# A two-layer decoder trunk on one core: another order of the opening, and other places for the modulation tiles

## The chip, the cores and the metric

One core of one Trainium2 chip runs the whole kernel. The metric is the device time of one execution in microseconds. Before the change the median of 3 runs was 2732.73 us (2731.3 to 2734.19).

## What is computed

1024 tokens of width 1024 pass two layers and a final RMSNorm; everything is float32. Cut to what matters here:

```python
c_act = silu(c)                                   # one vector of 1024
for l in range(2):
    mod = c_act @ w_ada[l] + b_ada[l]             # 6144 values per layer
    sh1, sc1, g1, sh2, sc2, g2 = split(mod, 6)
    h = rms_norm(x, ln1_g[l]) * (1 + sc1) + sh1
    z = h @ w_in[l]                               # pool input, q and kv latents, rope key, two gates
    y_a = pool_mixer(...) @ p_pool[l]
    y_b = mla(..., cos, sin) @ p_attn[l]          # 8 heads, causal
    x = x + g1 * ((sigmoid(gz_a) * y_a + sigmoid(gz_b) * y_b) @ w_out[l])
    h2 = rms_norm(x, ln2_g[l]) * (1 + sc2) + sh2
    x = x + g2 * (relu(h2 @ w_ff1[l])**2 @ w_ff2[l])
return rms_norm(x, final_g)
```

## The kernel before

Activations lie with the features on the 128 partitions: `x` is 8 tiles (k) of 128 x 1024, each in two halves c of 512 tokens. Every dense product is made of three TensorE (PE) matmuls per 128x128x512 block, since each operand is split into a high part (ScalarE cast, ACT) and a low part (a subtraction, mostly on VectorE, DVE): `split` (L305, L306) for activations, `w_split` (L254, L256) for weights. PE matmuls are recorded at L292, those of the second feed-forward product at L1235.

**Modulation tiles.** The 2 x 48 column groups of `w_ada` are tiles of 128x1024 (512 KB). `ada_tile` loads one (L472, on the queue of SyncE, SP) and multiplies and sums it with silu(c) in one DVE instruction (L474), which writes one column of `mod`; the tile's index j runs over sh1 (0 to 7), sc1 (8 to 15), g1 (16 to 23), sh2 (24 to 31), sc2 (32 to 39), g2 (40 to 47). `ada_pump(n)` takes the next n tiles from the list `adaq`; where it is called decides where the tiles stand.

**Queues and order.** SP's instructions stand in the order of the program, as all loads of weights, `x` and tiles do. The other engines are ordered by a scheduler, except inside `manual_schedule`. Buffers of 128x512 floats come from a ring `F` of 28 halves; a tile or a weight block takes two. A load waits on SP until the buffer's last reader is done, and the loads behind it wait too.

**The opening** (`start`): `x` for c = 0 (8 loads), then c, vectors, positions, 5 weight blocks, 16 tiles (those of sh1 and sc1 of layer 0), then `x` for c = 1. The squares of c = 0 are summed on DVE (L317); `rstd_ps` (L342 to L353) makes 1/rms. Per k the loop makes x times 1/rms on GpSimd (POOL, L666), two tiles and the scale on DVE (L474, L670), h's high part and value on ACT (L673, L674), and its low part on DVE for even k, on POOL for odd k (L676). Then the c = 1 half: `norm_tiles` (L378, L371) and at last `tables`, the sine and cosine tables (L510 to L566, mostly DVE; PE transposes them at L563).

**A layer.** Latents, rope key, pool mixer; the stage `m` of 8 steps (L973, L983 for m < NA = 4, L985 for m >= 4), with `attention_open` at m = 6; attention (scores, softmax at L1378 and L1422, left-over gate blocks at L1391); `w_out` (evacuated by `xupd`, L1062, and its squares L316, L317); then 8 feed-forward groups, of which the first 7 are `seven`: the first product with `ev` (L1155, L1156, `put` through L306), then products of prepared halves at L1235, evacuated at L1246. The calls of `ada_pump` before:

```python
            if l == 0:
                self.ada_pump(4)          # stage m, all 8 steps: 32 tiles, the rest of layer 0
        ...
            if b < 2:
                self.ada_pump(1)          # seven, first product: layer 1's tiles
            if i < 6:
                self.ada_pump(1)          # seven, second product
```

So layer 0 holds 32 tiles in stage m, 7 in group 0 and 8 in each of groups 1 to 5 (the last in group 6); layer 1 holds none.

## Time and profile before

| what | value |
|---|---|
| median of 3 runs | 2732.73 us |
| the profiled execution's own time | 2735.55 us |
| its span, first to last instruction | 2733.8 us |
| PE busy | 2603.5 us, 95% |
| DVE busy | 1891.6 us, 69% |
| ACT, POOL busy | 1186.2 us, 832.2 us |
| granted PE clock, mean | 0.986 of full speed |
| L474 (tiles) | 96 instructions, 147.3 us |

Busy time is the sum over an engine's instructions. The granted clock is the share of full speed that TensorE got. All sums below are made against the profiled execution; its time lies 2.8 us over the median.

### The profile page before, as it was taken

The numbers are of one execution on the slowest core, as the hardware profiler recorded it, in microseconds if no ns is written. First come the engines' busy times: TensorE is split into PE (matmuls) and PEld (weight loads), VectorE is DVE, ScalarE is ACT, GpSimd is POOL, SyncE is SP. The second block draws the span as 40 slices with busy tenths as digits, with TensorE's granted clock in tenths as the row PEclk, the third lists the DMA queues.
The fourth block names the chain that finished last, engine by engine and source line by source line (L and its number), as shares of the span: only waits on it lengthen the run. The fifth ranks groups of instructions, "written<-read, shape, count | busy, mean of one in ns | idle before, by whom it ended". The sixth has DMA issues, their size and how long they took to land.

```text
span 2733.8 us, 31817 instructions
## 1 busy us (share of the span) xinstructions
PE 2603.5 (95%) x11582; PEld 2141.9 (78%) x11582; DVE 1891.6 (69%) x2970; ACT 1186.2 (43%) x2215; POOL 832.2 (30%) x730
## 2 busy tenths in 40 slices
PE   3999879999989999999999999998999999999998
PEld 2788768888868777787888788887787888888887
DVE  8686467776697778777567644875758676676566
ACT  4433156663343333333335334665524343443332
POOL 5010011241054454544310201212303454544430
PEclk9999989999999999999999999999999999999999
DMA  6156555554032223222212624543810111111121
GB/s 232 64 208 237 183 134 128 138 197 169 31 111 71 90 106 124 91 79 84 86 70 82 237 84 120 145 121 103 290 54 16 47 62 62 58 43 39 50 74 62
DMA packets 121229, 299.69 MB, mean 110 GB/s; under 512 B 44016, under 2 KB 46192, under 8 KB 115952
## 3 DMA queue, kind: packets, MB, share of 16 engines
q1 hardware_dynamic: 105584, 236.83, 27.3%
q0 software_dynamic: 13472, 57.68, 5.5%
q10 hardware_dynamic: 2016, 3.15, 0.3%
q8 instruction: 91, 1.49, 0.2%
q14 instruction: 66, 0.54, 0.1%
HBM read 234.70 MB, written 62.91 MB: 109 GB/s over the span
## 4 chain that ended last, share of the span: by engine, by line
PE 72%; DVE 8%; DMA 4%; issue 2%; ACT 1%; POOL 0%; SPq 0%; DVEq 0%; ACTq 0%; POOLq 0%
PE b L292 61%; PE b L1235 11%; DVE rt L306 4%; DVE ft L1246 2%; DMA ft<-in_w_ada_dram 1%; DVE ft L474 1%; DMA ft<-in_w_ff_dram 1%; DMA mad<-ft 0%; DVE ft L1150 0%; DMA rt<-qrd 0%; DVE ft L1422 0%; ACT rt L305 0%; DMA zad<-ft 0%; DVE ft L743 0%; DMA ft<-mad 0%
## 5 line engine op out<-in xcount | busy, mean ns | idle before, releaser
L292 PE MATMUL b<-rt 128*128 128x512 f32 (+5 forms) x9160 | 2046.9, 385 | 73.0 <-ACT rt L305 16.3
L292 PEld LDWEIGHTS b<-rt 128*128 128x128 f32 (+1 forms) x9160 | 1689.2, 190 | 425.5 <-ACT rt L305 17.2
L306 DVE TENSOR_TENSOR rt<-ft,rt 128x256 fp32r<-128x256 f32 (+3 forms) x889 | 611.0, 720 | 164.7 <-ACT rt L305 123.6
L305 ACT CAST rt<-ft 128x512 fp32r<-128x512 f32 (+3 forms) x889 | 420.7, 501 | 483.5 <-POOL ft L1150 86.1
L1235 PE MATMUL b<-rt 128*128 128x512 f32 x2352 | 550.7, 393 | 27.7 <-DVE rt L306 14.7
L1235 PEld LDWEIGHTS b<-rt 128*128 128x128 f32 x2352 | 441.2, 189 | 132.7 <-DVE rt L306 21.6
L256 DVE TENSOR_TENSOR rt<-ft,rt 128x1024 fp32r<-128x1024 f32 (+2 forms) x127 | 160.2, 1265 | 151.8 <-ACT rt L254 148.9
L254 ACT CAST rt<-ft 128x1024 fp32r<-128x1024 f32 (+2 forms) x142 | 145.6, 1035 | 223.1 <-DMA ft<-in_w_ff_dram 122.3
L1246 DVE SCALAR_TENSOR_TENSOR ft<-b,mod,ft 128x512 f32<-128x512 f32 x280 | 204.5, 741 | 24.3 <-PE b L1235 24.3
L1150 POOL TENSOR_TENSOR ft<-ft 128x512 f32<-128x512 f32 x84 | 124.7, 1491 | 252.1 <-DVE ft L1156 184.4
L474 DVE CUSTOM_DVE_ANT_0 ft<-ft,cact,vecs 128x1024 f32<-128x1024 f32 x96 | 147.3, 1545 | 36.5 <-DMA ft<-in_w_ada_dram 36.5
L1156 DVE SCALAR_TENSOR_TENSOR ft<-b,ft 128x512 f32<-128x512 f32 x112 | 76.7, 687 | 84.3 <-ACT ft L1155 83.7
L1198 POOL TENSOR_TENSOR ft<-ft 128x256 f32<-128x256 f32 x56 | 50.3, 898 | 268.7 <-DVE rt L371 115.6
L1267 POOL TENSOR_TENSOR ft<-ft 128x512 f32<-128x512 f32 x56 | 91.5, 1635 | 78.0 <-DVE ft L1246 77.8
L1378 POOL PARTITION_ALL_REDUCE ft<-ft x32 | 64.3, 2009 | 154.4 <-DVE ft L1376 140.4
L1155 ACT ACTIVATE ft<-b 128x512 f32<-128x512 f32 x112 | 66.6, 596 | 102.1 <-PE b L292 101.6
L1423 ACT ACTIVATE ft<-ft 128x512 f32<-128x512 f32 x192 | 92.6, 519 | 36.1 <-DVE ft L1422 36.0
L1422 DVE TENSOR_TENSOR ft<-ft 128x512 f32<-128x512 f32 x192 | 96.8, 563 | 16.3 <-POOL ft L1378 16.3
L1276 POOL TENSOR_TENSOR ft<-ft 128x512 f32<-128x512 f32 x56 | 86.7, 1548 | 35.7 <-ACT ft L1274 35.5
L1208 POOL TENSOR_TENSOR ft<-ft 128x256 f32<-128x256 f32 x56 | 55.9, 999 | 123.6 <-DMA ft<-in_w_ff_dram 73.7
L1277 POOL TENSOR_TENSOR ft<-ft 128x512 f32<-128x512 f32 x56 | 86.9, 1552 | 1.0 <-DVE ft L1246 1.0
L316 ACT ACTIVATE ft<-ft 128x512 f32<-128x512 f32 x67 | 41.5, 630 | 79.7 <-DVE ft L1062 75.4
(153 smaller groups left out, 1515.0 us busy)
## 6 DMA issues: line engine op xcount, KB each, us to landing
ft<-in_w_ff_dram SPq DMA_DIRECT2D x128, 512.0 KB, 3.6
ft<-in_w_ada_dram SPq DMA_DIRECT2D x96, 512.0 KB, 4.5
ft<-in_w_in_dram SPq DMA_DIRECT2D x50, 512.0 KB, 5.5
ft<-in_x_dram SPq DMA_DIRECT2D x32, 256.0 KB, 3.8
qnd<-rt POOLq DMA_DIRECT2D x8, 1024.0 KB, 4.2
kd<-rt POOLq DMA_DIRECT2D x8, 1024.0 KB, 6.6
vd<-rt POOLq DMA_DIRECT2D x16, 512.0 KB, 6.9
mad<-ft POOLq DMA_DIRECT2D x16, 512.0 KB, 3.3
```

The lines of the kernel that those rows point to most:

```text
L254: nc.scalar.copy(h[:, :n], raw.ap[:, :n])
L256: eng.tensor_tensor(lo[:, :n], raw.ap[:, :n], h[:, :n].bitcast(F32), ALU.subtract)
L292: self.nc.tensor.matmul(ps, w, x, start=start, stop=stop)
L305: self.nc.scalar.copy(dst_h, src)
L306: self.nc.vector.tensor_tensor(dst_l, src, dst_h.bitcast(F32), ALU.subtract)
L474: nc.vector.tensor_tensor_reduce(out=r.ap, in0=r.ap, in1=self.cact, scale=1.0, scalar=self.vec("b_ada", col), op0=ALU.mult, op1=ALU.add, a ...
L1150: eng.tensor_tensor(out.ap, a.ap, b.ap, ALU.subtract)
L1235: nc.tensor.matmul(ps.ap, a, b, start=start and j + q == 0, stop=stop and j == 1 and q == 2, skip_group_check=True)
L1246: nc.vector.scalar_tensor_tensor(x, ps.ap, v, x, ALU.mult, ALU.add)
L1267: nc.gpsimd.tensor_tensor(x12, x12, u2.ap, ALU.add)
L1422: nc.vector.tensor_tensor(sl, sl, mb.ap[:, off:], ALU.subtract)
L1423: self.last_exp = nc.scalar.activation(sl, sl, AF.Exp, scale=SCALE)
```

## The change

The opening: c, then the vectors, then `x` for c = 0 are loaded first, then the tiles of k = 0 and 1, the five weight blocks, positions, the other 12 tiles, `x` for c = 1. The squares of c = 0 are summed by PE in a bank (8 matmuls with ones) and no longer on DVE. DVE follows the order of the program through all of `start` (`manual_schedule`), with the tiles of step k + 2 ahead of the low part of step k, and `tables` behind `norm_tiles`.

The layers: one list holds all 80 further tiles. Stage m pumps 4 tiles at m < 4 in both layers; `xupd` of `w_out` pumps one per evacuation (16) in both; `seven` pumps 3 in the first product of groups 1 to 5 and 1 in group 6, in layer 0 alone. Layer 0 so holds 16 + 16 + 16 tiles, layer 1 16 + 16.

```diff
@@ -636,49 +636,59 @@
         ones32 = t.ap[:, :P]
         posi = self.F.get(1)
 
-        def load_x(c):
+        def load_x(c, k):
             cs = slice(c * CH, (c + 1) * CH)
-            for k in range(KD):
-                self.x[k, c] = self.F.get(1)
-                nc.sync.dma_start(self.x[k, c].ap, A["x"][k][:, cs])
-
-        load_x(0)
+            self.x[k, c] = self.F.get(1)
+            nc.sync.dma_start(self.x[k, c].ap, A["x"][k][:, cs])
+
+        s1 = self.scl[:, 0:8]
+        sh1 = self.modc(0, 0)
+
+        def ada_pair(k):
+            if k < KD:
+                self.ada_tile(0, 8 + k)
+                self.ada_tile(0, k)
+                nc.vector.scalar_tensor_tensor(s1[:, k:k + 1], self.modc(0, 1)[:, k:k + 1], 1.0,
+                                               self.vec("ln1_g", k), ALU.add, ALU.mult)
+
         nc.sync.dma_start(cact, A["c"].broadcast_to([P, D]))
+        nc.scalar.activation(cact, cact, AF.Silu)
         nc.sync.dma_start(self.vecs, A["vecs"])
-        nc.sync.dma_start(posi.ap.bitcast(I32)[:, :8], A["positions"])
+        for k in range(KD):
+            load_x(0, k)
+        dve = tc.manual_schedule(engines={mybir.EngineType.DVE})
+        dve.__enter__()
+        ada_pair(0)
+        ps = self.B.get()
+        for k in range(KD):
+            t2 = self.F.get(1)
+            nc.scalar.activation(t2.ap, self.x[k, 0].ap, AF.Square)
+            self.mm(ps.ap, ones32, t2.ap, k == 0, k == KD - 1)
+            t2.free()
         rs = self.F.get(1)
-        for k in range(KD):
-            self.sq_add(rs.ap, self.x[k, 0].ap, k == 0)
-        self.rstd32(ones32, rs)
-        nc.scalar.activation(cact, cact, AF.Silu)
+        self.rstd_ps(ps, rs, D)
+        ada_pair(1)
         for k in range(5):
             self.lo_pool = k >= W_DVE
             self.w_load(True)
             self.w_split(True)
-        self.adaq = [(0, j) for j in range(16, 48)]
-        self.adaq1 = [(1, j) for j in range(48)]
-        s1 = self.scl[:, 0:8]
-        sh1 = self.modc(0, 0)
+        nc.sync.dma_start(posi.ap.bitcast(I32)[:, :8], A["positions"])
+        self.adaq = [(0, j) for j in range(16, 48)] + [(1, j) for j in range(48)]
         for k in range(KD):
-            if k == XK:
-                load_x(1)
             xr = self.F.get(1)
             nc.gpsimd.tensor_tensor(xr.ap, self.x[k, 0].ap, rs.ap, ALU.mult)
             self.x.pop((k, 0)).free()
-            self.ada_tile(0, 8 + k)
-            self.ada_tile(0, k)
-            nc.vector.scalar_tensor_tensor(s1[:, k:k + 1], self.modc(0, 1)[:, k:k + 1], 1.0,
-                                           self.vec("ln1_g", k), ALU.add, ALU.mult)
             hh, hl = self.act(self.h, k, 0)
             nc.scalar.activation(hh, xr.ap, AF.Identity, bias=sh1[:, k:k + 1], scale=s1[:, k:k + 1])
             nc.scalar.activation(xr.ap, xr.ap, AF.Identity, bias=sh1[:, k:k + 1], scale=s1[:, k:k + 1])
+            ada_pair(k + 2)
             eng = nc.gpsimd if k in H_POOL else nc.vector
             eng.tensor_tensor(hl, xr.ap, hh.bitcast(F32), ALU.subtract)
             xr.free()
         rs.free()
         acc1 = self.F.get(1)
-        if XK >= KD:
-            load_x(1)
+        for k in range(KD):
+            load_x(1, k)
         acc2 = self.F.get(1)
         for k in range(KD):
             a = acc2 if k in SQ_POOL else acc1
@@ -694,6 +704,7 @@
         for k in range(KD):
             self.x.pop((k, 1)).free()
         self.tables(ident, posi)
+        dve.__exit__(None, None, None)
         t.free()
         self.lo_pool = False
 
@@ -988,7 +999,7 @@
                 self.w_done("pp", l, m // 2)
             self.store.dma_start(self.mad[m], t.ap)
             t.free()
-            if l == 0:
+            if m < NA:
                 self.ada_pump(4)
         self.drop(yp)
 
@@ -1055,7 +1066,7 @@
         accs = [None] * NC
         xsrc = A["x"] if l == 0 else self.xd
 
-        def xupd(gv, last):
+        def xupd(gv, last, pump=False):
             def ev(m, c, ps):
                 cs = slice(c * CH, (c + 1) * CH)
                 xc = self.x[m, c].ap
@@ -1064,31 +1075,33 @@
                     if m == 0:
                         accs[c] = F.get(1)
                     self.sq_add(accs[c].ap, xc, m == 0)
+                if pump:
+                    self.ada_pump(1)
             return ev
 
         for k in range(KD):
             for c, r in enumerate(F.get(2).halves()):
                 self.x[k, c] = r
                 nc.sync.dma_start(self.x[k, c].ap, xsrc[k][:, c * CH:(c + 1) * CH])
-        s2 = self.scale_vec(l, 1, self.vec("ln2_g", l * KD, KD))
+        s2 = []
         sh2 = self.modc(l, 3)
 
         def post_o(b):
             if isinstance(b, tuple):
                 c = b[1]
                 self.drop(mg, c)
-                self.norm_x(c, accs[c], s2, sh2)
+                if c == 0:
+                    s2.append(self.scale_vec(l, 1, self.vec("ln2_g", l * KD, KD)))
+                self.norm_x(c, accs[c], s2[0], sh2)
 
         self.h = {}
-        self.dense([(("wo", l, m), 0, 1) for m in range(8)], (mg, KD), xupd(g1, True), head=3, tail=3,
+        self.dense([(("wo", l, m), 0, 1) for m in range(8)], (mg, KD), xupd(g1, True, True), head=3, tail=3,
                    post=post_o)
         hs = (self.h, KD)
 
 
         g2 = self.modc(l, 5)
         F.pack = False
-        if l + 1 < L:
-            self.adaq += self.adaq1
 
         def ev_f1(hid):
             def ev(m, c, ps):
@@ -1111,7 +1124,6 @@
             hid = {}
             self.dense([(("f1", l, 4 * g + m), 0, 1) for m in range(4)], hs, ev_f1(hid),
                        head=3 if g == 0 else 0)
-            self.ada_pump(8)
             last = g == 7
             if last:
                 self.drop(self.h)
@@ -1214,7 +1226,9 @@
                     q.free()
 
         def post(b):
-            if b < 2:
+            if l == 0 and 0 < g < 6 and b < 3:
+                self.ada_pump(1)
+            if l == 0 and g == 6 and b == 0:
                 self.ada_pump(1)
             if b == 1:
                 load(0)
@@ -1276,8 +1290,6 @@
                 nc.gpsimd.tensor_tensor(x22, x22, u3.ap, ALU.add)
                 nc.gpsimd.tensor_tensor(x21, x21, u3.ap, ALU.add)
                 u3.free()
-            if i < 6:
-                self.ada_pump(1)
             if i == 6:
                 n = self.wpos["f1", l, 4 * (g + 1)]
                 self.wlim = n + 1
```

Three places show how the instructions move. First the end of the opening on DVE. Before, the table's instructions (L525 to L551) stand among the square sums and the normalisation of c = 1 (L378, L371):

```order
L352 TENSOR_TENSOR sm<-sm 128x16
L531 CAST ft<-ft 128x256
L353 STREAM_TRANSPOSE ft<-sm 128x512
L532 TENSOR_TENSOR ft<-ft 128x256
L378 SCALAR_TENSOR_TENSOR ft<-ft,scl 128x512 x2
L538 TENSOR_TENSOR ft<-ft 128x128
L371 SCALAR_TENSOR_TENSOR rt<-ft,mod,rt 128x512
L378 SCALAR_TENSOR_TENSOR ft<-ft,scl 128x512
L540 TENSOR_TENSOR ft<-ft 128x128
L371 SCALAR_TENSOR_TENSOR rt<-ft,mod,rt 128x512
```

Now:

```order
L371 SCALAR_TENSOR_TENSOR rt<-ft,mod,rt 128x512
L378 SCALAR_TENSOR_TENSOR ft<-ft,scl 128x512
L371 SCALAR_TENSOR_TENSOR rt<-ft,mod,rt 128x512 x2
L510 CAST ft<-ft 128x8
L317 TENSOR_TENSOR ft<-ft 128x512
L512 TENSOR_TENSOR ft<-ft 128x128
L517 CAST rt<-ft 128x128
L518 TENSOR_TENSOR rt<-ft,rt 128x128
L525 TENSOR_SCALAR ft<-rt 128x128 x8
L527 TENSOR_SCALAR ft<-rt 128x128
L236 TENSOR_TENSOR rt<-ft,rt 128x8x32 x2
L530 CAST ft<-ft 128x1024
```

The table's instructions from L510 on now all stand behind the normalisation of c = 1, with weight splits (L236, L256) among them.

Second the start of `w_out` of layer 0 on DVE. L256 are weight splits, L1062 (now L1073) the evacuations of bank b into x, L317 the square sums. Before:

```order
L256 TENSOR_TENSOR rt<-ft,rt 128x1024 x3
L1062 SCALAR_TENSOR_TENSOR ft<-b_73,mod,ft 128x512
L1062 SCALAR_TENSOR_TENSOR ft<-b_74,mod,ft 128x512
L256 TENSOR_TENSOR rt<-ft,rt 128x1024
L1062 SCALAR_TENSOR_TENSOR ft<-b_77,mod,ft 128x512
L317 TENSOR_TENSOR ft<-ft 128x512 x2
L1062 SCALAR_TENSOR_TENSOR ft<-b_78,mod,ft 128x512
L1062 SCALAR_TENSOR_TENSOR ft<-b_71,mod,ft 128x512
L1062 SCALAR_TENSOR_TENSOR ft<-b_72,mod,ft 128x512
```

Now, with tiles (L474) ahead of and among the evacuations:

```order
L256 TENSOR_TENSOR rt<-ft,rt 128x1024 x3
L474 ISA ft,mod<-ft,cact,vecs 128x1024
L474 ISA mod 128x1
L1073 SCALAR_TENSOR_TENSOR ft<-b_73,mod,ft 128x512
L1073 SCALAR_TENSOR_TENSOR ft<-b_74,mod,ft 128x512
L474 ISA ft,mod<-ft,cact,vecs 128x1024
L474 ISA mod 128x1
L1073 SCALAR_TENSOR_TENSOR ft<-b_77,mod,ft 128x512
L317 TENSOR_TENSOR ft<-ft 128x512
L474 ISA ft,mod<-ft,cact,vecs 128x1024
L474 ISA mod 128x1
```

Three tiles are shown; four more follow before the next evacuation (bank b_78). 14 of the 16 stand ahead of the normalisation of c = 0, two behind it.

Third a feed-forward group of layer 0 on DVE. Before, tiles stand among the evacuations (L1246) and splits (L306) of the second product:

```order
L306 TENSOR_TENSOR rt<-ft,rt 128x256 x3
L474 ISA ft,mod<-ft,cact,vecs 128x1024
L474 ISA mod 128x1
L306 TENSOR_TENSOR rt<-ft,rt 128x256
L1246 SCALAR_TENSOR_TENSOR ft<-b_74,mod,ft 128x512
L306 TENSOR_TENSOR rt<-ft,rt 128x256 x3
L1246 SCALAR_TENSOR_TENSOR ft<-b_76,mod,ft 128x512
L474 ISA ft,mod<-ft,cact,vecs 128x1024
L474 ISA mod 128x1
L1246 SCALAR_TENSOR_TENSOR ft<-b_71,mod,ft 128x512
L306 TENSOR_TENSOR rt<-ft,rt 128x256 x4
L474 ISA ft,mod<-ft,cact,vecs 128x1024
```

Now the second product (L1260, was L1246) has none, and the next group's first product (L1168, was L1156) begins with three:

```order
L1260 SCALAR_TENSOR_TENSOR ft<-b_77,mod,ft 128x512
L1260 SCALAR_TENSOR_TENSOR ft<-b_78,mod,ft 128x512
L256 TENSOR_TENSOR rt<-ft,rt 128x1024 x2
L474 ISA ft,mod<-ft,cact,vecs 128x1024
L474 ISA mod 128x1
L474 ISA ft,mod<-ft,cact,vecs 128x1024
L474 ISA mod 128x1
L1168 SCALAR_TENSOR_TENSOR ft<-b_72,ft 128x512
L306 TENSOR_TENSOR rt<-ft,rt 128x256 x2
L474 ISA ft,mod<-ft,cact,vecs 128x1024
L474 ISA mod 128x1
```

The six tiles of the second product are gone and three stand at the start of the first.

## Rows read from the trace of the kernel before

**Rows 1.** the page's busy times by engine (us, share of the span, instructions)
```profile
PE 2603.5 (95%) x11582; PEld 2141.9 (78%) x11582; DVE 1891.6 (69%) x2970; ACT 1186.2 (43%) x2215; POOL 832.2 (30%) x730
```

**Rows 2.** the chain that ended last, layers 0 and 1: start us, us, what
```profile
814.73 43.56 PE b L292 x192
...
1327.33 177.62 PE b L292 x781
...
2140.63 42.39 PE b L292 x187
...
2630.23 85.91 PE b L292 x451
```

**Rows 3.** one line's instructions per layer: ns min/median/max, first and last start us
```profile
L973 ACT ACTIVATE ft<-b x8: 578/598/601, 231.4 to 286.1; 128x512 f32<-128x512 f32 x8
...
L973 ACT ACTIVATE ft<-b x8: 577/594/599, 1584.5 to 1640.6; 128x512 f32<-128x512 f32 x8
...
L1235 PE MATMUL b<-rt x1176: 386/389/632, 762.2 to 1326.9; 128*128 128x512 f32 x196
...
L1235 PE MATMUL b<-rt x1176: 387/389/629, 2095.0 to 2629.8; 128*128 128x512 f32 x196
```

**Rows 4.** windows, feed-forward: us, PE, PEld, DVE, ACT, POOL busy (count), PEclk, DMA, GB/s
```profile
944.00:988.60 44.60, 41.71 (x180) 33.25 (x179) 39.84 (x57) 15.43 (x32) 27.42 (x21) 1.00 0.37 132
...
988.60:1029.60 41.00, 41.00 (x182) 33.96 (x182) 27.21 (x36) 16.54 (x31) 16.77 (x14) 1.00 0.18 63
...
2222.20:2264.60 42.40, 42.40 (x189) 35.11 (x188) 21.04 (x30) 15.52 (x29) 15.27 (x13) 1.00 0.11 38
...
2264.60:2303.80 39.20, 39.20 (x175) 32.46 (x174) 33.53 (x48) 17.05 (x33) 26.14 (x22) 1.00 0.21 68
```

**Rows 5.** PE's waits, 250 to 370 us: total us, times, longest
```profile
PE b L292 <- ACT rt L305: 7.8, 1, 7.8
...
PE b L292 <- ACT ft L985: 7.2, 1, 7.2
```

**Rows 6.** line L474, 312 to 372 us: its instructions and what it waited for
```profile
L474 DVE CUSTOM_DVE_ANT_0 ft<-ft,cact,vecs x8: 1275/1285/2010, 319.8 to 361.7; 128x1024 f32<-128x1024 f32 x8
...
  DMA ft<-in_w_ada_dram: 13.6, 6
```

**Rows 7.** SP's waits, 250 to 370 us: total us, times, longest
```profile
SPq L472 <- DMA mad<-ft: 46.3, 5, 13.6
```

**Rows 8.** windows, the stage w_out of layer 0 (columns as in rows 4)
```profile
640.00:706.00 66.00, 66.00 (x293) 54.67 (x292) 27.14 (x33) 16.84 (x22) 0.00 (x0) 1.00 0.23 82
```

**Rows 9.** windows of the opening (columns as in rows 4)
```profile
0.00:20.00 20.00, 2.04 (x2) 0.50 (x2) 12.18 (x26) 14.44 (x18) 3.66 (x42) 1.00 0.90 325
...
60.00:80.00 20.00, 14.29 (x43) 9.46 (x44) 18.20 (x39) 8.06 (x15) 3.84 (x3) 0.83 0.04 8
```

**Rows 10.** line L474 in the opening, 0 to 62 us
```profile
L474 DVE CUSTOM_DVE_ANT_0 ft<-ft,cact,vecs x16: 1244/1280/2389, 24.0 to 58.5; 128x1024 f32<-128x1024 f32 x16
```

**Rows 11.** the timeline of the opening: start us, us, engine, line, operation
```profile
24.04 1.24 DVE L474 CUSTOM_DVE_ANT_0 ft<-ft,cact,vecs 128x1024 f32<-128x1024 f32 x1
...
59.67 0.69 DVE L676 TENSOR_TENSOR rt<-ft,rt 128x512 fp32r<-128x512 f32 x1
...
71.80 0.72 DVE L342 STREAM_TRANSPOSE ft<-b 128x512 f32<-128x512 f32 x1 [0.24 <-PE b L292]
...
95.85 2.13 PE L563 MATMUL b<-ft 128*128 128x128 f32 x16 [0.21 <-ACT ft L554]
```

**Rows 12.** the timeline of DVE: a 1/rms chain with POOL idle
```profile
731.60 0.72 DVE L342 STREAM_TRANSPOSE ft<-b 128x512 f32<-128x512 f32 x1 [5.45 <-PE b L292]
...
734.68 1.42 DVE L378 SCALAR_TENSOR_TENSOR ft<-ft,scl 128x512 f32<-128x512 f32 x2
```

**Rows 13.** windows, the start of attention in layer 0 (columns as in rows 4)
```profile
318.00:344.00 26.00, 15.54 (x65) 12.37 (x63) 11.28 (x24) 4.49 (x9) 1.12 (x2) 0.78 0.33 115
...
344.00:366.00 22.00, 8.28 (x26) 6.32 (x27) 19.80 (x37) 13.38 (x29) 3.78 (x3) 0.66 0.47 135
```

## The prediction, made before the changed kernel ran

> **What bounds the kernel now.** The page's first part says that PE is busy for 95% of the span [rows 1], so a gain can come only from the places where PE still waits. To find them I compared the two layers, which do the same work, except that all tiles behind the opening (80 of 96) stand in layer 0. The chain of waits gives the first measure: from the start of the first product of group 1 to that of group 7 layer 0 takes 1327.33 - 814.73 = 512.6 us, layer 1 2630.23 - 2140.63 = 489.6 us [rows 2]. Then I took fixed instructions per layer by their lines [rows 3]. From the first sigmoid of stage m (L973) to the start of group 7 layer 0 takes 1327.3 - 231.4 = 1095.9 us, layer 1 2630.2 - 1584.5 = 1045.7 us. The difference of **50.2 us** splits into four stretches:
>
> - Stage m < 4 (first to last L973): 54.7 against 56.1 us, so -1.4, although layer 0 has tiles here.
> - Last L973 to the first product of group 0 (L1235), which is the rest of stage m, attention, merge, w_out and the first half of group 0: 476.1 against 454.4, so 21.7.
> - From there to the start of group 1: 814.7 - 762.2 = 52.5 against 45.6, so 6.9.
> - Groups 1 to 6: 23.0.
>
> The windows say why the groups cost. In layer 0's second product DVE is busy 39.84 of 44.60 us, and PE waits for what is left; in layer 1 it is busy 33.53 of 39.20 us and PE is busy all the time [rows 4]. Six tiles of 1.28 us make 7.7 us, about what DVE has too much. In the first product of the same groups DVE is far from full: 27.21 of 41.00 us in layer 0 (with two tiles), 21.04 of 42.40 in layer 1, PE busy throughout in both [rows 4].
>
> The start of attention costs for another reason. PE stands there for 7.8 and 7.2 us at a time [rows 5], while DVE has the last eight tiles between 319.8 and 361.7 us and waits 13.6 us for their transfers [rows 6]. Those tiles' loads stand on SP behind buffers that the stores of stage m free late: 46.3 us of waiting [rows 7].
>
> **The change, part by part.** *Tiles taken away.* The change takes the tiles out of m >= 4, out of group 0 and out of every second product. If the rest is free, layer 0 runs like layer 1 now: **-50.2 us**. I count the difference between the layers and not PE's idle time, since attention already filled part of those waits with other work.
>
> *Tiles left in m < 4 of layer 0, and 16 new ones there in layer 1.* The nearest row is the same stage of layer 0, which with tiles takes 1.4 us less than layer 1 without. The load queue is the same as before up to the 16th tile, and in layer 1 the weights of this stage are the same. I take 0; the ends are 0 and 3 us, for a late weight block or two.
>
> *16 tiles in w_out, in both layers.* Cover: in 66 us of this stage of layer 0 PE is busy for 66.00 and DVE for 27.14 [rows 8], so DVE has 38.9 us free, and the 14 tiles ahead of the normalisation take 14 x 1.28 = 17.9. But DVE takes them in the order shown, ahead of evacuations, and so it waits for their transfers too. x holds 16 of the 28 halves of the ring, and the allocator has four or five free ones at these calls, so two tiles alternate between two buffers. One tile in single file took (361.7 - 319.8) / 7 = 6.0 us [rows 6]; two in flight make 3.0 us each, 14 x 3.0 = 42 us, which fits into 66. Queued behind a waiting tile are an evacuation and a square sum; PE does not feel it until its 8 banks are full, and in this stage a bank lasts 24 x 0.227 = 5.4 us (43.56 us / 192 matmuls [rows 2]). Without that cover (one buffer alone) it is 14 x 6.0 = 84 us against 66, thus 18 us late per layer. Two tiles stand behind the first normalisation, where DVE waits for PE anyway (5.45 us, first of [rows 12]). I take 1.5 us per layer, 3 in all; ends 0 and 18 for both together, since half of the loss above would be met by free banks.
>
> *15 tiles in the first product of groups 1 to 5, one in group 6.* Three tiles are 3.8 us on a DVE that idles for 42.40 - 21.04 = 21.4 us there [rows 4]. The third load stands ahead of the second load of w_ff2 on SP; prepared halves that come late would show as before. I take 1 us for all; the ends are 0 and 5 x 4.1 = 20 us, the whole of today's excess per group (85.7 against 81.6 us; 85.7 is 988.60 - 902.90, two windows of one group [rows 4], 81.6 is 489.6 / 6).
>
> Sum of the layers: -50.2 + 0 + 3 + 1 = **-46 us**.
>
> *The opening.* The tiles run on DVE from 24.04 us on, and the last low part of c = 0 starts at 59.67 [rows 11]: 35.6 us for 16 tiles, single ones between 1.24 and 2.39 us long [rows 10]. In the new order c, x for c = 0 and two tiles are the first 3.7 MB; at the 325 GB/s of the first 20 us [rows 9] they are there at some 11.3 us, with the start of the queue at 12.8 (an estimate). So DVE can begin 11.2 us earlier. From this go the 1/rms chain behind the first pair, 734.68 - 731.60 = 3.1 us where nothing disturbs it [rows 12], and two weight splits that stood ahead of the tiles, 2.4 us. The squares of c = 0 leave DVE and come on ACT and PE, which have nothing else then. What is left is 5.7 us: low parts end at 54 us. Before, 12.1 us went from there to the transpose of the second 1/rms (71.80 [rows 11]), with table instructions in between; now four square sums (2.8 us) and POOL's last low part stand there, some 6 us. The transpose then starts at 60, **12 us earlier**.
>
> Then the tables take most of it back. Until now DVE makes them in the gaps, and PE transposes them at 95.85 us, 36.2 us behind the last low part [rows 11]; DVE is nearly full in between (18.20 of 20 us [rows 9]). The new order leaves it the same instructions, square sums, normalisation, table and splits, but the 33 of the table at the end: 54 + 36 = 90, and 1 us for POOL's last low part, 91 us. The normalisation of c = 1 is done long before: 3.1 us of chain and 16 instructions of 0.71 us (1.42 us for two [rows 12]) end at 60 + 14.5 = 74.5, PE's matmuls on it and on the rope key some 4 us later. So PE stands for about 12 us before the transposes. What counts for the rest of the kernel is when PE gets past them: 95.9 - 91 = 4.9 us earlier.
>
> PE's pause has a second price. In the pauses at the start of attention the granted clock fell to 0.78 and 0.66 [rows 13], so part of the matmuls ran at 1.2 in place of 2.4 GHz: 65 matmuls in 15.54 us and 26 in 8.28, where full speed needs 0.227 each. That is 0.8 and 2.4 us too much; I take 1.6 for this pause. The Trainium skill ("TensorE: Matmul & The Clock Gate", section "HAM oscillation — how this bites in real kernels") speaks against the change here: a wait between two bursts drops the clock, and the next burst starts at half speed. Priced at half speed throughout, the 26 matmuls would lose 5.9 us, and the opening would win nothing. The row has both levels in one window, so I keep 1.6.
>
> Opening: -4.9 + 1.6 = **-3 us**; ends -10 (tiles undisturbed by POOL) and +5 (the first pair late, the tables with every split waiting).
>
> **Sum.** -46 - 3 = -49 us against 2735.55, thus 2686.5; the profiled execution lies 2.8 us over the median, so I forecast **2684 us** for the median. Below, faster and slower mean by more than 0.2%, which is what a measurement of this kernel can tell from no change.
>
> **Rivals.** A: *the moved tiles still cost in the feed-forward groups and w_out.* For it: DVE is in order, its tiles stand ahead of evacuations, and buffers are scarce. Against it: PE is busy throughout in the first product of layer 0 with two tiles per group. If the upper ends come, 18 + 20 in place of 4, it gives 2684 + 34 = 2718; with half of that 2701. Chance 0.2.
>
> B: *the opening loses.* Tables behind everything on DVE and PE in order: if they end at 101, not 91, the kernel takes 2694. Chance 0.13.
>
> C: *the difference of the layers is not the tiles'.* Only groups 1 to 6 are shown to be DVE's; the 21.7 us around attention might be another order of left-over gate blocks. Then -23 - 7 + 4 - 3 = -29, thus 2704. Chance 0.05.
>
> D, slower: *tiles stop PE in w_out*, through the two buffers. At the start of attention eight tiles cost 21.7 us, 2.7 each. At this price the 28 tiles of w_out cost 76 us: 2684 + 76 = 2760. It decides from 49 / 28 = 1.75 us of PE's time per tile on. Against it stand the 38.9 us free on DVE and 8 banks. Chance 0.04.
>
> The forecast has the other 0.58. That the tiles do not move is excluded by the order shown.
>
> **How the numbers follow.** Its own range is 2674 to 2694 (opening from -10 to +3, layers 3 either way). For 8 in 10 I add B and the lower half of A, to 2708, and leave -60 as the lower end, 2672. Slower 0.04 is D; the same 0.02 is the far end of A; faster 0.94.
>
> **What would show it.** Right: second products of layer 0 at 39 to 40 us with PE busy throughout, no wait of PE over 3 us between 280 and 370 us, the first and last start of L1235 in layer 0 some 536 us apart, as in layer 1 (2629.8 - 2095.0 = 534.8 [rows 3]), transposes of the tables near 91 us behind a pause of PE of some 12 us. Wrong: waits of PE for evacuations in w_out, DVE waiting for tiles there for over 10 us, or a transpose at 100 us.

## The result, and the profile after

The changed kernel takes **2665.75 us** (median of 4 runs, 2663.97 to 2669.83), the kernel before beside it 2733.19 us (2731.3 to 2734.19): a ratio of 0.976, 95% interval 0.9748 to 0.9772. I had forecast 2684, with a range of 2672 to 2708. The direction was right; the gain is 67 us in place of 49. The profiled execution took 2669.83 us, its span 2668.1.

The page's busy times of the changed kernel, as in [rows 1]: PE has the same work but for the squares of c = 0, and the span has shrunk around it.

```profile
PE 2590.3 (97%) x11596; PEld 2142.9 (80%) x11596; DVE 1857.4 (70%) x2963; ACT 1185.0 (44%) x2214; POOL 812.9 (30%) x730
```

The two lines of [rows 3] per layer: the sigmoids of stage m (L973, now L984), and the second feed-forward products (L1235, now L1249).

```profile
L984 ACT ACTIVATE ft<-b x8: 579/598/600, 243.0 to 297.7; 128x512 f32<-128x512 f32 x8
...
L984 ACT ACTIVATE ft<-b x8: 578/597/600, 1530.1 to 1586.2; 128x512 f32<-128x512 f32 x8
...
L1249 PE MATMUL b<-rt x1176: 388/389/505, 739.7 to 1271.9; 128*128 128x512 f32 x196
...
L1249 PE MATMUL b<-rt x1176: 388/389/797, 2029.3 to 2563.8; 128*128 128x512 f32 x196
```

With the first product of the merge (the multiplication in `ev_pa`, L1041 before, now L1052) as one more mark, here for layer 0 and layer 1 before and then now, the two profiled executions split as in the table below.

```profile
L1041 DVE TENSOR_TENSOR ft<-b,ft x16: 675/679/692, 589.6 to 636.3; 128x512 f32<-128x512 f32 x16
...
L1041 DVE TENSOR_TENSOR ft<-b,ft x16: 675/680/693, 1921.2 to 1970.4; 128x512 f32<-128x512 f32 x16
...
L1052 DVE TENSOR_TENSOR ft<-b,ft x16: 676/678/692, 566.5 to 614.0; 128x512 f32<-128x512 f32 x16
...
L1052 DVE TENSOR_TENSOR ft<-b,ft x16: 676/678/692, 1857.1 to 1903.9; 128x512 f32<-128x512 f32 x16
```

| stretch | before, us | after, us | difference | forecast |
|---|---|---|---|---|
| start to the last sigmoid, layer 0 | 286.1 | 297.7 | +11.6 | -1.6 |
| attention, layer 0: last sigmoid to first merge product | 303.5 | 268.8 | -34.7 | -21.7 |
| merge and w_out, layer 0, to the first product of group 0 at L1235 | 172.6 | 173.2 | +0.6 | +1.5 |
| feed-forward, layer 0: first to last L1235 | 564.7 | 532.2 | -32.5 | -28.9 |
| to the last sigmoid of layer 1 | 313.7 | 314.3 | +0.6 | 0 |
| attention, layer 1 | 280.6 | 270.9 | -9.7 | 0 |
| merge and w_out, layer 1 | 173.8 | 172.2 | -1.6 | +1.5 |
| feed-forward of layer 1, and the rest | 638.8 | 638.8 | 0.0 | 0 |

(The first row of the forecast is the opening's -3 and the +1.4 of stage m < 4; the fifth lies between the layers.) Two things stand out. The opening lost where I had it win, and attention gained some 23 us more than I had, 10 of them in layer 1, where the tiles of the forecast could bring nothing at all.

What attention of layer 0 gained can be read from PE. From the last sigmoid to the first merge product PE was busy for 276.88 of 303.5 us before, and it is now for 266.93 of 268.8. So 24.7 us of the gain are waiting that is gone. The other 10.0 us are the same 1284 matmuls taking less time: the granted clock of the stretch was 0.94 before and is 1.00 now. The start of the stretch, where [rows 13] has the pauses and clocks of 0.78 and 0.66, now looks like this (columns as in [rows 4]):

```profile
297.70:330.00 32.30, 32.30 (x144) 26.68 (x143) 6.11 (x8) 9.96 (x18) 2.66 (x5) 1.00 0.49 155
330.00:360.00 30.00, 30.00 (x154) 25.81 (x152) 21.66 (x51) 20.22 (x45) 5.12 (x4) 1.00 0.39 97
```

What came out as forecast are the feed-forward groups. These windows are the first and the second product of one group of layer 0, as in [rows 4]:

```profile
945.93:988.32 42.39, 42.39 (x189) 35.10 (x188) 22.78 (x35) 14.98 (x29) 14.73 (x14) 1.00 0.21 75
988.32:1027.53 39.21, 39.21 (x174) 32.47 (x174) 35.39 (x48) 16.66 (x33) 23.93 (x21) 1.00 0.19 68
```

PE is busy in both all the time, and the group takes 81.60 us, what a group of layer 1 took before. In `w_out` of layer 0 DVE now has 43.42 us of work in 66 where [rows 8] had 27.14, and PE has its 66.00 of 66 as before:

```profile
617.00:683.00 66.00, 66.00 (x293) 54.66 (x292) 43.42 (x62) 16.34 (x22) 0.00 (x0) 1.00 0.54 186
```

DVE waits 7.8 us for tiles in this window, in eight pieces of at most 2.2 us, and PE stays busy throughout.

The opening is another matter. In the timeline (start us, us, engine, line, operation) the first tile is on DVE at 12.81, the last low part of c = 0 at 59.60, the second 1/rms at 68.48, and PE's transposes at 102.63, behind a wait of 12.27 us; [rows 11] had 24.04, 59.67, 71.80 and 95.85.

```profile
12.81 1.28 DVE L474 CUSTOM_DVE_ANT_0 ft<-ft,cact,vecs 128x1024 f32<-128x1024 f32 x1 [9.60 <-DMA ft<-in_w_ada_dram]
...
49.30 1.27 DVE L474 CUSTOM_DVE_ANT_0 ft<-ft,cact,vecs 128x1024 f32<-128x1024 f32 x1
...
59.60 0.68 DVE L686 TENSOR_TENSOR rt<-ft,rt 128x512 fp32r<-128x512 f32 x1
...
68.48 0.72 DVE L342 STREAM_TRANSPOSE ft<-b 128x512 f32<-128x512 f32 x1 [2.08 <-PE b L292]
...
102.63 3.67 PE L563 MATMUL b<-ft 128*128 128x128 f32 x16 [12.27 <-ACT ft L554]
105.95 23.20 PE L292 MATMUL b<-rt 128*128 128x512 f32 x96
```

So the tiles began 11.2 us earlier and ended as late as before. The tile at 49.30 is the eleventh; in the kernel before the eleventh starts at 50.33. The transposes after the wait take 3.67 us where [rows 11] has 2.13.

### The profile page after: what moved, and what is told of

Read it like the earlier page. It is cut to its first block, busy times and chain, and to the rows that moved or that the text cites. A ratio compares the mean times of both kernels' runs of the same rounds, so it can differ in the third digit from the quotient of the medians.

```text
span 2668.1 us, 31812 instructions
## 1 busy us (share of the span) xinstructions
PE 2590.3 (97%) x11596; PEld 2142.9 (80%) x11596; DVE 1857.4 (70%) x2963; ACT 1185.0 (44%) x2214; POOL 812.9 (30%) x730
## 4 chain that ended last, share of the span: by engine, by line
PE 85%; DVE 6%; DMA 4%; issue 3%; ACT 1%; POOL 0%; SPq 0%; DVEq 0%; POOLq 0%; ACTq 0%
PE b L292 65%; PE b L1249 19%; DVE rt L306 1%; DVE ft L474 1%; DMA ft<-in_w_ada_dram 1%; DMA ft<-zbd 1%; DMA ft<-mad 0%; DVE rt L256 0%; ACT rt L254 0%; DMA vd<-rt 0%; DMA ft<-in_w_out_dram 0%; DVE scl L651 0%; DVE ft L1053 0%; DMA ft<-in_w_ff_dram 0%; ACT rt L305 0%
## 5 line engine op out<-in xcount | busy, mean ns | idle before, releaser
L306 DVE TENSOR_TENSOR rt<-ft,rt 128x256 fp32r<-128x256 f32 (+3 forms) x889 | 601.4, 709 | 163.3 <-ACT rt L305 120.5
L1249 PE MATMUL b<-rt 128*128 128x512 f32 x2352 | 542.7, 391 | 4.6 <-DVE rt L306 2.6
L1249 PEld LDWEIGHTS b<-rt 128*128 128x128 f32 x2352 | 442.6, 189 | 100.1 <-DVE rt L306 5.4
L256 DVE TENSOR_TENSOR rt<-ft,rt 128x1024 fp32r<-128x1024 f32 (+2 forms) x127 | 160.9, 1268 | 197.7 <-ACT rt L254 195.0
L1260 DVE SCALAR_TENSOR_TENSOR ft<-b,mod,ft 128x512 f32<-128x512 f32 x280 | 205.5, 741 | 34.3 <-PE b L1249 34.1
L1162 POOL TENSOR_TENSOR ft<-ft 128x512 f32<-128x512 f32 x84 | 125.2, 1498 | 291.7 <-DVE ft L1168 223.5
L474 DVE CUSTOM_DVE_ANT_0 ft<-ft,cact,vecs 128x1024 f32<-128x1024 f32 x96 | 130.0, 1365 | 38.2 <-DMA ft<-in_w_ada_dram 38.1
L1210 POOL TENSOR_TENSOR ft<-ft 128x256 f32<-128x256 f32 x56 | 48.8, 872 | 309.5 <-DVE rt L371 230.5
L1168 DVE SCALAR_TENSOR_TENSOR ft<-b,ft 128x512 f32<-128x512 f32 x112 | 76.7, 687 | 89.4 <-ACT ft L1167 88.9
L1281 POOL TENSOR_TENSOR ft<-ft 128x512 f32<-128x512 f32 x56 | 95.1, 1702 | 82.4 <-DVE ft L1260 57.2
L1290 POOL TENSOR_TENSOR ft<-ft 128x512 f32<-128x512 f32 x56 | 75.2, 1343 | 27.6 <-ACT ft L1288 27.5
L1388 DVE TENSOR_TENSOR ft<-ft 128x512 f32<-128x512 f32 (+3 forms) x128 | 64.6, 504 | 16.6 <-ACT ft L1379 9.8
L1291 POOL TENSOR_TENSOR ft<-ft 128x512 f32<-128x512 f32 x56 | 76.0, 1358 | 0.0
```

The costliest lines, as they stand in the source:

```text
L256: eng.tensor_tensor(lo[:, :n], raw.ap[:, :n], h[:, :n].bitcast(F32), ALU.subtract)
L306: self.nc.vector.tensor_tensor(dst_l, src, dst_h.bitcast(F32), ALU.subtract)
L474: nc.vector.tensor_tensor_reduce(out=r.ap, in0=r.ap, in1=self.cact, scale=1.0, scalar=self.vec("b_ada", col), op0=ALU.mult, op1=ALU.add, a ...
L1162: eng.tensor_tensor(out.ap, a.ap, b.ap, ALU.subtract)
L1249: nc.tensor.matmul(ps.ap, a, b, start=start and j + q == 0, stop=stop and j == 1 and q == 2, skip_group_check=True)
L1260: nc.vector.scalar_tensor_tensor(x, ps.ap, v, x, ALU.mult, ALU.add)
```

## Experiments

Each run's time is a median of 4 to 12 executions and is set against the kernel before on the same chip; stages are read from one profiled execution each. The changed kernel itself shared a chip only with runs 9 to 11 (as run 12). "Last sigmoid" below is the last start of the sigmoids of stage m in layer 0, by which the opening's loss or gain has arrived: 286.1 us before, 297.7 changed. It varies between executions: with the old opening (before, runs 2 to 4) it lies between 284.6 and 288.7, with the new one (changed, runs 1 and 12) between 295.3 and 297.7.

**1. The opening alone** (the new `start`; the calls of `ada_pump` as before).

```diff
 # start() of the changed kernel, but (code cut; the calls in the layers are those of before)
-        self.adaq = [(0, j) for j in range(16, 48)] + [(1, j) for j in range(48)]
+        self.adaq = [(0, j) for j in range(16, 48)]
+        self.adaq1 = [(1, j) for j in range(48)]
```

> The changed opening alone, with all tiles of the layers where they were before. Theory 1 (the opening itself loses, and nothing gives it back): the first sigmoid of layer 0 starts near 243 us, as in the changed kernel (before: 231.4), and the time is 2744 us (2740 to 2747). Theory 2, the forecast on record: the opening wins 3 us, 2730. Theory 3 (the late opening is made up in attention, where PE waits anyway): first sigmoid at 243, time 2733.

Measured: 2728.88 us against 2731.04, ratio 0.9987 (0.9976 to 0.9998). None of the three: the opening does lose, for the last sigmoid stands at 295.7 us, 9.6 late, but the time is not longer (2 us less, and the interval ends just under 1). Layer 1 gave the loss back, though not a tile in it had moved: its attention takes 270.3 us (before 280.6, changed 270.9).

**2. The layers alone** (the old `start`, the list `adaq` and the calls of the changed kernel).

> The opening of the kernel before, with the tiles of the layers in their new places. Theory 1 (opening and layers add up): 2666 - 11.6 = 2654 us (2650 to 2658), faster than both kernels. Forecast on record: the layers are worth 46 us, 2687. Theory 3 (part of the gain of the layers comes from the late opening): 2662 to 2668, the time of the changed kernel.

Measured: 2657.36 us, ratio 0.9724 (0.9702 to 0.9746). Last sigmoid at 284.6, attention 269.4 and 271.3 us. Theory 1: this is 8 us faster than the changed kernel, which therefore owes nothing to its new opening. (Run 10, the same with the transposes moved, is 11 us faster than run 12, the changed kernel, on one chip.) The layers are worth 74 us, not 46.

**3. Only the 16 tiles of m >= 4 of layer 0 moved, into `w_out` of layer 0.** The code is cut; as in the change, `scale_vec` moves behind the tiles that it reads.

```diff
-            if l == 0:
+            if l == 0 and m < NA:
                 self.ada_pump(4)
...
+                if pump and l == 0:      # xupd, w_out of layer 0
+                    self.ada_pump(1)
```

> The kernel before, with one edit: the 16 tiles of m >= 4 of layer 0 go into w_out of layer 0. All tiles of layer 1 stay in the feed-forward groups of layer 0. Theory 1 (those tiles cost the attention of layer 0 what it gained, 43.6 us without the 6.9 of group 0, and layer 1 loses its weight split ahead of the last maximum on POOL by the new order): 2733 - 36.7 - 11.6 = 2685 us, with groups 1 to 6 of layer 0 still at 512.6 us. Forecast on record (layer 1 as floor): 21.7 us less 1.5 for w_out, 2713. If layer 1's gain belongs to its own tiles, it isn't here: 2696, with layer 1's last sigmoid to group 1 at 500 us.

Measured: 2688.49 us, ratio 0.9841 (0.982 to 0.9863): 43 us won by this edit alone, within 4 us of theory 1. The marks of layer 0:

```profile
L973 ACT ACTIVATE ft<-b x8: 579/598/601, 233.1 to 287.9; 128x512 f32<-128x512 f32 x8
...
L1041 DVE TENSOR_TENSOR ft<-b,ft x16: 653/678/694, 558.0 to 604.7; 128x512 f32<-128x512 f32 x16
```

Attention of layer 0 takes 270.1 us, so these 16 tiles alone cost it 33.4 us, and their new place in `w_out` nothing (172.6 us, as before). PE is busy for 267.20 us of it at a clock of 1.00. The view of PE's waits shows none between 280 and 380 us, where the kernel before has the 7.8 and 7.2 of [rows 5] and, in the same view, 6.6, 2.6 and 0.4 more. The feed-forward of layer 0 keeps 561.8 us, as it keeps its tiles. Layer 1's attention has dropped to 272.6 us here too, so its gain does not belong to the tiles of layer 1.

**4. Layer 1's attention: a weight split behind the last exponential.** From its last sigmoid to group 0 PE has one long wait in the kernel before (us in total, times, longest):

```profile
PE b L292 <- ACT rt L305: 8.5, 1, 8.5
```

Where it comes from can be read on POOL. This is its timeline there, at the end of attention:

```profile
1895.79 2.38 POOL L256 TENSOR_TENSOR rt<-ft,rt 128x1024 fp32r<-128x1024 f32 x1 [7.43 <-ACT ft L1391]
1903.91 1.80 POOL L1378 PARTITION_ALL_REDUCE ft<-ft  x1 [5.75 <-issue]
...
1923.23 7.99 POOL L256 TENSOR_TENSOR rt<-ft,rt 128x1024 fp32r<-128x1024 f32 x3 [10.68 <-DMA ft<-in_p_attn_dram]
```

The scheduler had put the first weight split of the merge (L256) ahead of the last unit's maximum (L1378). Behind it POOL stands for 5.75 us that no wait explains. What stands there is shown by the view of that line over layer 1: a configuration instruction, four records before, up to 1898.4, and two after, both at the start of attention.

```profile
L1378 POOLq MODIFY_POOL_CONFIG  x4: 7/22/37, 1669.9 to 1898.4; - x4
```

```profile
L1390 POOLq MODIFY_POOL_CONFIG  x2: 37/37/37, 1615.5 to 1615.6; - x2
```

The chain view of the kernel before has such a stand ahead of the split as well, behind the split's own configuration instruction at 1888.4:

```profile
1889.84 5.40 issue
...
1898.41 5.50 issue
```

With the split of 2.38 us the two make 13.3 us. The maximum on DVE that the last unit waits for had ended at 1889.53 (the 1893.4 of the expectation below is the end of another instruction).

In the changed kernel the maximum starts at 1831.87 and the split behind it:

```profile
1831.87 1.77 POOL L1390 PARTITION_ALL_REDUCE ft<-ft  x1 [3.09 <-DVE ft L1388]
...
1845.97 2.54 POOL L256 TENSOR_TENSOR rt<-ft,rt 128x1024 fp32r<-128x1024 f32 x1 [11.03 <-PE b L292]
```

The edit makes this order in the kernel before:

```diff
-        self.w_pump(self.wpos["pa", l, 0])
+        with self.tc.issue_after(self.last_exp.ins):
+            self.w_pump(self.wpos["pa", l, 0])
```

> The kernel before, with one edit: the weight split ahead of the merge is issued behind the last exponential of attention, so that POOL has it behind its last maximum in layer 1 too. Theory 1 (in layer 1 POOL loads the code of the split and that of the maximum again, 5.75 us of issue behind a split of 2.4 us, while PE waits 8.5 us): POOL goes from DVE's maximum (1893.4 us) at once to the last unit's, 8 to 12 us earlier, and the time is 2723 us (2720 to 2726); layer 0 is unchanged. Rival (the wait goes elsewhere: PE then waits for the split, which comes later): 2731 to 2735.

Measured: 2728.84 us, ratio 0.9988 (0.9975 to 1.0): between the two expectations. The extra configuration changes are gone (two in place of four), and the last maximum starts 249.0 us after the last sigmoid (before 1903.91 - 1640.6 = 263.3; 245.7 to 245.9 in the changed kernel and runs 1 and 3). Of these 14.3 us the merge starts 5.8 earlier: attention takes 274.8 us, and where PE waited 8.5, 1.3 and 1.2 us from the last sigmoid to group 0 it now waits 4.6 and 0.3. So by this one execution the split is a part of it, 6 of 10 us; the other part came with the new order as a whole, and which instruction carries it I have not separated. As a whole time this edit is at the limit of what can be told from no change.

**5 to 7. The opening, one cause at a time.** Each is the changed kernel with one edit. Run 5 leaves DVE's order alone and moves PE's transposes behind work that needs no table:

```diff
 # tables() ends before the transposes; these are tables_pe(), called in layer 0 behind the rope key's weights
+            with self.tc.issue_after(self.last_mm.ins):   # last matmul of the first five blocks
+                self.tables_pe()
```

> The changed kernel, with one edit: the 16 transposes of the tables are issued behind the first five blocks of w_in and the rope key of both halves, so that PE does not stand in front of them while DVE finishes the tables. DVE's order is unchanged. Theory 1 (the opening loses by PE's order: 96 matmuls that need no table stand behind the transposes): the wait of 12.3 us falls under 2 us, the first sigmoid starts at 231 to 233 us in place of 243, and the time is 2656 us (2653 to 2659). Rival (who waits for the tables then is the rope on DVE, and PE for its banks): first sigmoid at 240 to 243 us, 2663 to 2668.

Measured: 2660.48 us, ratio 0.9735 (0.972 to 0.9751), last sigmoid at 285.5: 12.2 us earlier than in the changed kernel, and where it was before the change. The transposes are at 111.97 us now, later than ever, and no wait of PE stands ahead of them. Transposes and sigmoids, then all that PE still waits for from 60 to 135 us:

```profile
111.97 1.91 PE L568 MATMUL b<-ft 128*128 128x128 f32 x16
...
L993 ACT ACTIVATE ft<-b x8: 579/598/601, 233.4 to 285.5; 128x512 f32<-128x512 f32 x8
...
PE b L292 <- ACT rt L305: 4.8, 1, 4.8
PE b L292 <- ACT rt L381: 2.5, 1, 2.5
PE b L292 <- DVE rt L306: 1.4, 1, 1.4
```

The stage says theory 1. The median lies 4 us above its 2656 and between the two ranges, so the time alone does not decide.

Run 6 lets the scheduler order DVE again behind the last low part of c = 0, and so puts the tables' instructions between those of the normalisation:

```diff
+        dve.__exit__(None, None, None)
         acc1 = self.F.get(1)
...
         self.tables(ident, posi)
-        dve.__exit__(None, None, None)
```

> The changed kernel, with one edit: DVE's written order ends behind the last low part of c = 0, so that the tables' instructions stand between those of the normalisation of c = 1, as before the change. Theory 1 (tables behind everything leave DVE's gaps of 60 to 68 us empty, 0.35 + 1.43 + 2.08 = 3.9 us): the tables end 4 us earlier, PE's wait for them falls from 12.3 to 8 us, and the time is 2662 us (2659 to 2664). Rival 1 (it was the low part of c = 0 coming late that set the tables' end; the order behind it is worth nothing): 2664 to 2668. Rival 2 (between the normalisation's instructions the tables delay that, and PE waits there in place of here): PE's waits up to 110 us keep their sum, 2664 to 2668.

Measured: 2660.56 us, ratio 0.9743 (0.9727 to 0.9759); the wait in front of the transposes is 3.0 us and not 8, and the last sigmoid comes 6.6 us earlier. Theory 1, with more in it than the gaps of DVE that I had counted: the transposes come at 99.64 us, 3.0 earlier, and behind the shorter wait they take 2.13 us in place of 3.67, and the 96 matmuls behind them 22.05 in place of 23.20.

Run 7 takes POOL's work beside the tiles away: its three weight splits (`W_DVE`), its low parts (`H_POOL`) and the products with 1/rms go to DVE. POOL keeps its square sums of c = 1.

```diff
-W_DVE = 2
-H_POOL = (1, 3, 5, 7)
+W_DVE = 5
+H_POOL = ()
...
-            nc.gpsimd.tensor_tensor(xr.ap, self.x[k, 0].ap, rs.ap, ALU.mult)
+            nc.vector.tensor_tensor(xr.ap, self.x[k, 0].ap, rs.ap, ALU.mult)
```

> The changed kernel, with one edit: POOL has no work beside the tiles of the opening. The three weight splits, the eight products of x with 1/rms and the four low parts of c = 0 that POOL had are DVE's. Theory 1 (an instruction of DVE is stretched by one of POOL that runs at the same time): the twelve tiles behind 20 us take 1.27 us each (now 2.3 in eight of them), the sums behind them 0.15 us; of some 16 us of stretching go 3 x 1.2 + 8 x 0.69 + 4 x 0.68 = 11.8 us of new work, so that the last low part of c = 0 ends 4 us earlier than 60.9, the transposes come 4 us earlier, and the time is 2662 us (2659 to 2664). Rival (the stretching comes from the transfers into the same memory): the tiles keep 2.3 us, the low part comes 12 us later, and the time is 2674 to 2680.

Measured: 2659.19 us, ratio 0.9733 (0.9717 to 0.9749), last sigmoid at 293.4, 4.3 us earlier, in an execution that took 7 us more than the median. The views of the tiles' line and of the sums behind them, 20 to 62 us (ns min/median/max), first of the changed kernel, then of run 7:

```profile
L474 DVE CUSTOM_DVE_ANT_0 ft<-ft,cact,vecs x14: 1244/1774/3347, 20.2 to 58.3; 128x1024 f32<-128x1024 f32 x14
...
L651 DVE SCALAR_TENSOR_TENSOR scl<-mod,vecs x7: 148/1214/2318, 23.6 to 59.5; 128x1 f32<-128x1 f32 x7
```

```profile
L474 DVE CUSTOM_DVE_ANT_0 ft<-ft,cact,vecs x14: 1244/1280/2309, 19.9 to 49.3; 128x1024 f32<-128x1024 f32 x14
...
L651 DVE SCALAR_TENSOR_TENSOR scl<-mod,vecs x7: 149/155/157, 22.3 to 51.5; 128x1 f32<-128x1 f32 x7
```

An instruction on one column takes 0.155 us alone and up to 2.32 beside POOL. The transfers, the rival, were not fewer: 242 GB/s from 20 to 60 us, in the changed kernel 240. The two tiles that still take 2.3 us in run 7 start at 47.05 and 49.29, beside POOL's square sums of c = 1 (46.74 to 50.51). The wait in front of the transposes stays at 12.2 us (they come 5.3 us earlier, and so does all that is ahead of them); run 5's cause and this one are separate.

By their medians runs 5, 6 and 7 are one (2659.2 to 2660.6 us), and their intervals touch that of the changed kernel. What tells them apart, and shows each cause, are the stages. Run 7's 4.3 us at the last sigmoid are of the size of that mark's spread; its reading rests on the durations of the tiles and sums and on the transposes.

**8 and 11. Both edits** (runs 5 and 7 together), on two chips.

> The two edits together: transposes of the tables behind the first five blocks of w_in, and no work of POOL beside the tiles. If each theory holds: no wait for the tables, low parts 4 us earlier, first sigmoid at 228 to 231 us, 2652 us (2648 to 2656). If the transposes' place alone counts: 2655 to 2658. If neither: 2664 to 2668.

> The kernel with both edits again, beside the changed kernel on the same chip: 2653 us (2650 to 2656), 12 to 13 us under the changed kernel.

Measured: 2653.37 us, ratio 0.971 (0.9696 to 0.9725), and again 2646.7, ratio 0.9692 (0.9677 to 0.9707). The first is as expected; the second is 3 us under its range, and 21 and not 12 to 13 under the changed kernel (run 12). Last sigmoid at 280.2 and 277.9 us: now the opening does win, 6 to 8 us on the kernel before.

**9. The squares of c = 1 on PE as well**, the sums of DVE and POOL replaced by eight matmuls with ones.

> The kernel with both edits (transposes later, no work of POOL beside the tiles), and the squares of c = 1 summed by PE as those of c = 0 are: seven sums leave DVE and POOL. Theory 1 (DVE's chain sets the opening): the two tiles that POOL's sums still stretch take 1.3 us, four sums of 0.69 us go, the transpose of the second 1/rms comes 5 us earlier than 63.4, the first sigmoid at 223 to 225 us, and the time is 2648 us (2645 to 2651). Rival (the eight matmuls take PE 16 x 0.6 = 9.6 us that c = 0's blocks need): 2652 to 2657.

Measured: 2645.14 us, ratio 0.9683 (0.967 to 0.9696). The 1/rms of c = 1 came as expected, at 57.58 us, but the first sigmoid stands at 230.4 and not at 223 to 225 (run 11: 225.8). The last did not move (279.1), and the time, though in the range of theory 1, is that of run 11. DVE's chain no longer sets the opening's end; what does is open.

**10. The old opening with the transposes later**, on top of run 2.

> The opening of before with the tiles of the layers in their new places, and the transposes of the tables behind the first five blocks of w_in. Before's opening shows a wait of 0.2 us ahead of the transposes, so by theory 1 (the place of the transposes matters only where DVE is late) the time stays at 2657 us (2654 to 2660). Rival (the place is worth something by itself, for instance 4 us of clock): 2650 to 2653.

Measured: 2656.85 us, ratio 0.9725 (0.9711 to 0.9738), run 2's time: theory 1. In these runs the place of the transposes is worth something only where DVE is late.

**12. The changed kernel again.**

> The changed kernel again, for the comparison on one chip: 2666 us (2663 to 2669), first sigmoid at 243 us.

Measured: 2668.02 us, ratio 0.977 (0.9752 to 0.9788), first sigmoid at 240.1, last at 295.3. Runs 9 and 11 beat it on the same chip by 21 to 23 us, and both beat the kernel before by 84 to 85.

## Why the prediction was right, and where it was wrong

**Right: the tiles in the feed-forward groups.** The 23.0 us of groups 1 to 6 came out to the tenth: a group of 81.60 us with PE busy throughout. The tiles at the start of them cost 0 and not 1 us. Group 0 gave 9.5 us where 6.9 were forecast (739.7 to 782.73 us in place of 762.2 to 814.73).

**Right: `w_out`, and so rival D wrong.** 16 tiles took no time from PE in either layer (+0.6 and -1.6 us for the whole stretch; 3 forecast). Run 3 says it for layer 0 by itself.

**Wrong by 13 us in layer 0 and 10 in layer 1: "if the rest is free, layer 0 runs like layer 1 now".** That step took layer 1 as the floor, since it had no tiles. It had a loss of its own, the 8.5 us of PE's waiting at the end of attention; I had read PE's waits only around layer 0's attention. Run 1 shows that this loss goes without a tile of layer 1 being moved, run 4 that a weight split ahead of the last maximum on POOL is more than half of it. So the level to compare with was 269 to 273 us (both layers of the changed kernel and of run 3), not 280.6. Both layers came down to it, and the 21.7 us of the tiles at the start of attention were 33 (run 3). The sign stood in layer 0 itself: PE idled for 26.6 us in this stretch (303.5 less 276.88), and its matmuls took 10.0 us more at a clock of 0.94 than they do at 1.00. The difference between the layers, which I took in place of these figures, hid a third of the loss. Rival C had doubted this term in the other direction: not the tiles', therefore not gained.

**Wrong in sign: the opening, -3 forecast, +11.6 measured (rerun: +9.2); rival B, with its transpose behind 101 us, came true.** The step that failed is "what is left is 5.7 us: low parts end at 54 us". The first pair was on DVE at 12.8 us to the tenth. But I let the 35.6 us of the old tile stretch simply start earlier. Its tiles were not limited by DVE alone: POOL's products and splits run in the same 30 us, and DVE's instructions wait beside them until POOL is through with its products, at 48 us before and 49 us after. The lead of 11.2 us at the first tile was 1.0 at the eleventh. Run 7 takes POOL's part away, and the transposes come 5.3 us earlier. That the durations of one line ran from 1.24 to 2.39 us stood in [rows 10], and I read it as scatter.

A second term failed behind it: "54 + 36 = 90", the table's instructions in 36 us wherever they stand. From the last low part (59.60) to the transposes (102.63) it is 43.0 us, where the kernel before has 36.2. Put behind everything, they leave DVE idle before the normalisation (1.43, 0.35 and 2.08 us between 60 and 69 us). Run 6 lets them back between, and it is 39.2 us. Together the two terms put the transposes 11.6 us behind the 91 of the forecast.

Right in this part were the 14.4 us from the second 1/rms to the end of the normalisation (14.5 forecast), the wait ahead of the transposes (12.3, forecast 12), and a slow clock behind it: granted 0.61 in the window after the wait, that is a mean between 1.2 and 2.4 GHz, with 3.67 us for transposes that took 2.13 and 23.20 for 96 matmuls that took 22.07, 2.7 us in all (1.6 forecast). Behind these matmuls the changed kernel is 8.8 us late; the last 2.8 of the 11.6 come after them, run 12 does not have them, and their cause is open.

```profile
86.50:102.60 16.10, 3.85 (x16) 2.87 (x16) 12.56 (x27) 6.22 (x9) 0.00 (x0) 0.76 0.10 36
102.60:110.00 7.40, 7.37 (x29) 6.59 (x30) 0.00 (x0) 4.30 (x8) 0.00 (x0) 0.61 0.44 162
```

One more reading was wrong. I priced PE's wait by when the transposes come. Run 5 has them 9 us later still and wins 12 us, for it was not the tables that PE lacked: 96 matmuls stood behind the transposes in its order and need none.

**The sum.** The time lies below the range because of the attention terms. Against a forecast of -49.2 the first stretch of the table was 13.2 us worse, the two attentions 22.7 better, the rest of the layers 7.0 better: -65.7 between the spans. Two misses of opposite sign made the time look nearer than the steps were: with the opening as forecast the time would have been some 13 us further below the range. That is luck.

## What to carry to other kernels

A stage without the suspect is not yet a floor: look for its own waits before you take a difference for a cost, and check it by an edit that moves the suspect and nothing else. Where an engine is fed earlier, ask which engine runs beside it and paces it; here the line whose durations spanned a factor of two was waiting for that engine. And where an in-order engine stands before something late, moving that thing behind independent work can be worth more than making it early (run 5 against run 6: 12.2 and 6.6 us at the last sigmoid).

## What the runs showed of the hardware

**An instruction of DVE waited for the one that POOL had under way.** With POOL idle a tile takes 1.28 us, beside POOL's products 2.3 to 3.35. The Trainium skill ("SBUF — State Buffer", section "Who interferes with whom") says that a DVE instruction with two SBUF inputs contends with a GpSimd instruction that reads SBUF, and that one of them waits for the whole of the other. Run 7 agrees for the tiles, and for the one-column sums, whose 0.155 us became up to 2.32. Such a sum of the changed kernel, begun at 23.58 us, ends at 25.90, when the weight split that POOL began at 23.20 ends (25.89):

```profile
23.58 2.32 DVE L651 SCALAR_TENSOR_TENSOR scl<-mod,vecs 128x1 f32<-128x1 f32 x1
...
23.20 2.69 POOL L256 TENSOR_TENSOR rt<-ft,rt 128x1024 fp32r<-128x1024 f32 x1 [0.63 <-DMA ft<-in_positions_dram]
```

Whether DVE holds POOL up as well, no run separates.

**A change to another kind of instruction on POOL cost up to 5.75 us.** Between a weight split and the next cross-partition maximum stood 5.75 us of issue in layer 1 of the kernel before, and 5.74 ahead of the first maximum of its layer 0, each behind the configuration instruction (at 1898.4 and 337.7 us); ahead of the split it was 5.40. Where POOL waits longer for something else it costs nothing: in layer 0 of the changed kernel the instruction is at 326.9 us, and the maximum waits for DVE until 333.61.

```profile
343.41 1.80 POOL L1378 PARTITION_ALL_REDUCE ft<-ft  x1 [5.74 <-issue]
...
L1378 POOLq MODIFY_POOL_CONFIG  x2: 42/42/42, 337.7 to 337.7; - x2
```

The Trainium skill ("GPSIMD Engine Reference", section "1.1 Terminology") says that this instruction loads a library of code at run time; its section "2.1 Instruction dispatch" gives approximately 6 us for the first call behind such a load. The trace agrees, with 5.4 to 5.75 us.

**One kernel, two medians 6.7 us apart** (runs 8 and 11, on two chips; the kernel before moved by 1 us between the same two). The single executions overlap (2648.3 to 2655.06 and 2644.27 to 2653.14 us), so whether the chip is the reason is not shown. Edits to the opening that differ by less than that are told apart here by their stages, not by the time.
